# A layer kernel: the down product's first input group split early, its sevens begun later, and one transposed block of x moved by GpSimd's DMA queue

## The chip, the cores and the metric

The kernel runs on one core of one Trainium2 chip. The metric is the device time of one execution in microseconds (us). TensorE (PE) multiplies matrices, VectorE (DVE), ScalarE (ACT) and GpSimd (POOL) work on elements, and SyncE (SP) issues most of the DMAs. Each engine works through its own queue in order; an instruction at the head of a queue that waits for a semaphore holds up all that stands behind it.

## The reference

One layer of a hybrid encoder: SEQ = 256 rows, D_MODEL = 2048, D_FF = 5632, all in float32, batch and depth 1. What matters here are the two half feed-forward products:

```python
def swiglu(h, w_gate, w_up, w_down):
    return (jax.nn.silu(h @ w_gate) * (h @ w_up)) @ w_down

x = x + 0.5 * swiglu(rms_norm(x, ffn1_norm), ffn1_w_gate, ffn1_w_up, ffn1_w_down)
h = rms_norm(x, mix_norm)
proj = h @ w_in              # u | q | k | v
...                          # state space group, attention group, output projection: x += ...
x = x + 0.5 * swiglu(rms_norm(x, ffn2_norm), ffn2_w_gate, ffn2_w_up, ffn2_w_down)
gate = sigmoid(rms_norm(x, ple_norm) @ w_ple_gate)
e = (p @ w_ple_proj) * gate
x = x + rms_norm(e, ple_post_norm)
```

## The kernel before

**Products in three passes.** Each float32 operand is split in a rounded high part (hi, by a copy on ScalarE, L168) and the rest (lo, by a subtract on VectorE, L171). A product is hi by hi, lo by hi and hi by lo, all summed in PSUM: lines L286, L287 and L291 of `gemm_half`, twelve matmuls of 128x512 for a "half" (two row blocks of 128 of the weights, both blocks of 128 rows of x). The names in the profile are whi and wlo for weights, nhi, nlo, hhi, hlo for activations, ahi, alo for prepared quarters. Weights come in tiles of 1 MB (`raw`, three buffers, issued by SP at L275), each of which feeds two halves.

**Gate and up.** `ffn` runs over 11 blocks of 512 hidden columns (f = 0 to 10). A block multiplies x by w_gate and w_up; the later blocks (`pair`) form the first quarter of the inner dimension by a scheme of seven quarter products ("sevens", L301 and L305) instead of eight, from weights in the tiles dg and du, and the rest plainly in `rest`. The end of a pair is L523 (VectorE adds the up sums from PSUM) and L526 (times the gate). The result is turned by a 32x32 transpose on VectorE (L203, into `mid`) and written by sixteen small DMAs of SP (`turn_quarters`, L217) to a tensor `hidden` in DRAM, from which the down product reads it transposed.

**Down.** The third product of the feed-forward multiplies the 5632 hidden columns, in 11 groups of 512, by w_down, for two pairs of column blocks of x (p = 0 and 1). `seven` names the groups that go by sevens, (0, 4) and (0, 4, 7); the others are plain, in an order where both blocks of the pair (c = 0, 1) take each group in turn, except for the last `cut` groups: those go through c = 0 first and then backward through c = 1. Group 1 is thus the first plain group. For a plain group `act` loads the hidden values (hf, L582) and splits them into hhi and hlo; only two groups are held, so some are read again in the backward part. `left` (L617 and splits) prepares the quarters of hidden values for the sevens, `right` (L629, tiles up and low) the weights. The units of the sevens are spread between the plain halves, from half `lead` to half `span`; `merge` adds their sums to x. When a block of x is done (L719), `nxt.block` prepares it for the next stage.

**The next stage's input.** `Normed.block` squares x for the norm (L404) and, for the first three of four blocks, turns it: VectorE transposes (L203, `mid`), sixteen small DMAs of SP move the 32-row strips (L217, h<-mid), and `parted` splits the turned block by ScalarE (nhi, L178) and VectorE (nlo, L180). The last block is transposed by TensorE (L387). After the first product the next stage is the input projection w_in, which runs beside loads for the state space part (L991, six tiles of 512 KB); after the second it is w_ple_gate.

**The order.** `put_off(n, fn)` traces a function n steps later; every half is a step. The program is traced in that order; a planner then places the instructions in each engine's queue by its own estimate of when their inputs are ready, with the traced order as the priority, and inserts the semaphores. So an instruction can stand in a queue at another place than its line suggests; only instructions marked with `pin` keep behind what was traced before them on their engine. Tiles of one tag share a fixed number of buffers (bufs); a new one waits until an older one has been read for the last time. hhi and hlo have two buffers; in the first feed-forward these also hold t1, t2, t4 and kept of a pair, in the second the first two blocks of x.

Of the kernel before, what the change touches and what calls it, by code (L numbers as in the profile page):

```python
# [26 lines left out]
NB = 512  # L27
# [6 lines left out]
def layer_kernel(ctx: ExitStack, tc: tile.TileContext, a: dict, shapes: dict, out: bass.AP):  # L34
# [61 lines left out]
    def start(g):  # L96
        beside.append(g)
        return g
# [106 lines left out]
            src.rearrange("p (f q b) -> p f q b", f=nk, q=4),  # L205
        )

    def turn_quarters(out, mid, steps):

        def g():
            for _ in range(steps):
                yield
            for i in range(4):
                for q in range(4):
                    nc.sync.dma_start(  # L217
                        out[32 * q : 32 * q + 32, :, i], mid[32 * i : 32 * i + 32, q]
                    )
                yield  # L220

        return start(g())
# [135 lines left out]
    class Normed:  # L358
# [8 lines left out]
            self.ss = [small(ND) for _ in range(TT)]  # L367
            self.r = None

        def block(self, n, steps=(6, 11)):  # L370
            if self.laid:
                ps = self.laid(n)
            elif n < self.early:

                mid = com("mid")[:, :1024].rearrange("p (q t f b) -> p q t f b", q=4, t=TT, b=32)
                out = com("h")
                for t in range(TT):
                    turn_blocks(mid, xt[t][n], t, 0, 4)
                turn_quarters(out.rearrange("p (t i f b) -> p t i f b", t=TT, i=4, f=4), mid, steps[0])
                put_off(steps[1], self.parted, n, out.rearrange("p (g f b) -> p f g b", f=4, b=32))  # L380
                put_off(1, self.squares, n)
                return
            else:
                ps = aux()
                for t in range(TT):
                    for j in range(4):
                        pin(nc.tensor.transpose(  # L387
                            ps[:, j * T + t * P : j * T + (t + 1) * P], xt[t][n][:, j * P : (j + 1) * P], ident
                        ))
            self.parted(n, ps.rearrange("p (j s) -> p j s", j=4))  # L390
            if not self.laid:
                put_off(1, self.squares, n)
# [30 lines left out]
    def ffn(i, xn, nxt, bg=None):  # L423
# [21 lines left out]

        first_pair = (early if bg else 0) + 1
        spare = "h" if bg else "n"
        left, right = [], {}

        def fetch(f, steps=6):  # L450


            def g():
                dg, du = (
                    get(hp, s, 4 * NB).rearrange("p (j n) -> p j n", j=4) for s in ("dg", "du")
                )
                for d, w in ((dg, wg), (du, wu)):
                    nc.sync.dma_start(d, w[:NB, f * NB : (f + 1) * NB].rearrange("(j p) n -> p j n", p=P))
                b11, b21, b12, b22 = dg[:, :2], dg[:, 2:], du[:, :2], du[:, 2:]
                t1, t2, t4, kept = (  # L460
                    actp.tile([P, 1024], F32, tag=spare + s, name=uid("t"), bufs={"n": 4, "h": 2}[spare])
                    for s in ("hi", "lo", "hi", "lo")
                )
                t1, t2, t4 = (t.rearrange("p (j n) -> p j n", j=2) for t in (t1, t2, t4))
                right[f] = b11, b21, b22, t1, t2, b12, t4, kept
                for _ in range(steps):
                    yield
                for o, x, y in ((t1, b12, b11), (t2, b22, t1), (b12, b22, b12), (t4, b21, t2)):
                    nc.vector.tensor_tensor(out=o, in0=x, in1=y, op=ALU.subtract)
                    yield  # L470

            start(g())

        def rest(ps, w, f, starts):
            for k0 in range(4, KD, 4):
# [8 lines left out]
        def pair(f, prefetch):  # L484

            (a11, a12, a22), (s1, s2, s3, s4) = left[0]
            b11, b21, b22, t1, t2, t3, t4, kept = right.pop(f)
            x, a, y = acc(), acc(), acc()
            o6, o7 = kept[:, :NB], kept[:, NB:]
            o1, o5 = get(hp, "o1", NB), get(hp, "o5", NB)  # L490
            todo = [
                (x, s2, t2, o6), (a, a11, b11, o1), (y, s1, t1, o5), (x, s3, t3, o7), (a, a12, b21, None),
                (y, s4, b22, None), (x, a22, t4, None),
            ]
            runs = []
            for i, (ps, l, r, o) in enumerate(todo):
                while len(runs) < min(i + 3, len(todo)):
                    n = len(runs)
                    runs.append(product(*todo[n][:3], todo[n][3] is not None and n != 3))
                runs[i]()  # L500
                if o is not None:
                    nc.scalar.copy(o, ps)
                if i % 2 or i == 6:
                    step()
            if prefetch:
                fetch(f + 1)

            def sums():
                nc.vector.tensor_tensor(out=o6, in0=o6, in1=o1, op=ALU.add)
                nc.vector.tensor_tensor(out=o7, in0=o7, in1=o1, op=ALU.add)  # L510
                nc.vector.tensor_tensor(out=o7, in0=o7, in1=o5, op=ALU.add)

            put_off(3, sums)
            rest([a, x], wg, f, ())
            sg = com("sg")
            nc.scalar.activation(sg[:, :NB], a, AF.Silu, scale=xn.rs(0))
            nc.vector.tensor_tensor(out=sg[:, NB:], in0=x, in1=o1, op=ALU.add)
            nc.scalar.activation(sg[:, NB:], sg[:, NB:], AF.Silu, scale=xn.rs(1))
            z = acc()
            rest([y, z], wu, f, (1,))  # L520
            hh = com("h")
            for ps, o in ((y, o6), (z, o7)):
                nc.vector.tensor_tensor(out=o, in0=ps, in1=o, op=ALU.add)  # L523
            for t, o in enumerate((o6, o7)):
                sl = slice(t * NB, (t + 1) * NB)
                nc.vector.scalar_tensor_tensor(  # L526
                    out=hh[:, sl], in0=o, scalar=xn.rs(t), in1=sg[:, sl], op0=ALU.mult, op1=ALU.mult
                )
            put_off(2, turned, hp, f, hh)
# [40 lines left out]
            put_off(2, turned, hp, f, hh)  # L570

        pools.close()
        down(wd, hT, nxt)

    def down(w, hT, nxt):

        nk = F // P // 4
        kept = {}
# [44 lines left out]
        def right(pool, g, n0):  # L623
# [16 lines left out]
            start(g_())  # L640
            return b

        with phase("down") as pool:
            for p in range(ND // 2):
                seven = ((0, 4), (0, 4, 7))[p]
                n0 = 2 * p * NB
                banks = []
                begun = set()
                v1, v7, v6, v5 = (u[:, c * NB : (c + 1) * NB] for u in (aux(), aux()) for c in range(2))
                plain = [g for g in range(nk) if g not in seven]  # L650
                cut = len(plain) - (4 if p else 2)
                order = [(g, c) for g in plain[:cut] for c in range(2)]
                order += [(g, 0) for g in plain[cut:]] + [(g, 1) for g in plain[cut:][::-1]]
                ready, acts = {}, {}

                def units(g):

# [23 lines left out]

                work = all_units()
                n_units, done, halves_done = 7 * len(seven), 0, 0
                lead, span = 4, (28, 22)[p]
                if p == 0:
                    left(pool, seven[0])
                ready[seven[0]] = right(pool, seven[0], n0)
                banks += [acc() for _ in range(4)]
                for g, c in order:
                    if g not in acts:  # L690
# [4 lines left out]
                    for half in list(weight_halves(w, 4 * g, 4, n0 + c * NB)):  # L695
                        keys = (2 * c, 2 * c + 1)
                        starts = tuple(t for t in range(TT) if keys[t] not in begun)
                        begun.update(keys)
                        gemm_half(
                            [banks[k] for k in keys], (acts[g], half), range(TT), starts, end and half[0] == 1,  # L700
                            skip_group_check=True,
                        )
                        step()
                        halves_done += 1
                        due = min(n_units, max(0, (halves_done - lead) * n_units // (span - lead)))
                        while done < due:
                            next(work)
                            done += 1
                            if done % 7 == 2 and done // 7 + 1 < len(seven):
                                ready[seven[done // 7 + 1]] = right(pool, seven[done // 7 + 1], n0)  # L710
                            if (p, done) in ((0, 1), (1, 7)):
                                left(pool, seven[done // 7 + 1])
                            if done == n_units:
                                finish(work)
                                merge(p, v1, v7, v6, v5)
                    if end:
                        n = 2 * p + c
                        for t in range(TT):
                            nc.vector.scalar_tensor_tensor(  # L719
                                out=xt[t][n], in0=banks[2 * c + t], scalar=0.5, in1=xt[t][n], op0=ALU.mult, op1=ALU.add  # L720
                            )
                        put_off(0, nxt.block, n, (4, 9)) if n == ND - 2 else put_off(2, nxt.block, n)

    def merge(p, v1, v7, v6, v5):

# [795 lines left out]
```

## Time and profile before

| | before |
|---|---|
| median of 3 runs | 1892.97 us (1892.61 to 1893.03) |
| the profiled execution | 1891.06 us |
| its span, first to last instruction | 1889.3 us |
| TensorE busy | 1868.1 us, 99% of the span |
| VectorE busy | 1412.9 us, 75% |
| ScalarE busy | 1068.8 us, 57% |
| GpSimd busy | 30.6 us, 2% |
| DMA | 425.65 MB, mean 225 GB/s |
| mean granted clock of TensorE | 0.996 |

Times in the profile's rows are counted from the span's start. A row of the timeline gives start, duration, engine, line, operation, out<-in, shape and count, and in brackets how long the engine stood idle before it and which instruction released it. "SPq" is the issue of a DMA by SP, not its transfer. The first product's down stage begins at 495 us and ends at 736 us, the second product's begins at 1539 us and ends at 1779 us.

### The profile page before, as it was taken

To read this page: it belongs to the slowest core of one execution; us is meant where nothing else is said; L and a number is where in the kernel's file an instruction comes from. 1 tells how busy PE (TensorE), PEld (TensorE's weight loads), DVE (VectorE), ACT (ScalarE), POOL (GpSimd) and SP (SyncE) were. 2 spreads that over 40 slices of the span, in tenths; PEclk is the share of its full clock that TensorE was granted. 3 is DMA by queue.
4 is the path that set the end of the run, shared out by engine and by line. 5 is a ranking of instruction groups with operands and counts; after the bars stand their busy time and mean duration, and the time that the engine had idled before them with its cause. 6 is when DMAs were issued, how large, how long until landed. Compare 5 with 4: busy or idle time off the path is not lost.

```text
span 1889.3 us, 24210 instructions
## 1 busy us (share of the span) xinstructions
PE 1868.1 (99%) x8998; PEld 1539.4 (81%) x8998; DVE 1412.9 (75%) x1898; ACT 1068.8 (57%) x1325; POOL 30.6 (2%) x48
## 2 busy tenths in 40 slices
PE   9999999999999999999999999999999999999998
PEld 7888888888788887888898888888888877888886
DVE  8985766777778886686566877777777778888755
ACT  7456665555455665455785555555555545566654
POOL 0000000000000000010010000000000000000000
PEclk9999999999999999999999999999999999999999
DMA  8777877675887757675547556666656588775653
GB/s 322 233 241 251 270 245 246 203 237 175 281 279 269 237 178 257 232 250 189 199 136 255 192 199 202 220 223 200 201 179 229 174 281 280 272 235 190 226 201 122
DMA packets 268214, 425.65 MB, mean 225 GB/s; under 512 B 17728, under 2 KB 88640, under 8 KB 267968
## 3 DMA queue, kind: packets, MB, share of 16 engines
q1 hardware_dynamic: 255472, 409.06, 65.2%
q10 hardware_dynamic: 12624, 15.04, 2.2%
q8 instruction: 70, 1.15, 0.2%
q14 instruction: 48, 0.39, 0.1%
HBM read 392.59 MB, written 26.21 MB: 222 GB/s over the span
## 4 chain that ended last, share of the span: by engine, by line
PE 95%; DMA 2%; DVE 1%; ACT 1%; issue 0%; SPq 0%; DVEq 0%; ACTq 0%
PE acc L286 26%; PE acc L287 26%; PE acc L291 26%; PE acc L301 6%; PE acc L305 3%; PE aux L301 2%; PE aux L305 1%; DMA hf<-hidden 1%; DMA rot<-scr_rot 0%; PE aux L1008 0%; DVE wlo L171 0%; PE acc L1287 0%; PE acc L1278 0%; PE acc L1282 0%; DMA raw<-in_w_in 0%
## 5 line engine op out<-in xcount | busy, mean ns | idle before, releaser
L168 ACT CAST whi<-raw 128x1024 fp32r<-128x1024 f32 x570 | 595.0, 1053 | 536.6 <-PE acc L287 421.1
L171 DVE TENSOR_TENSOR wlo<-raw,whi 128x1024 fp32r<-128x1024 f32 x570 | 687.5, 1222 | 250.7 <-ACT whi L168 250.0
L286 PE MATMUL acc<-whi,nhi 128*128 128x512 f32 x1504 | 590.6, 393 | 5.6 <-ACT whi L168 4.8
L287 PE MATMUL acc<-whi,nlo 128*128 128x512 f32 x1504 | 586.5, 390 | 0.0
L291 PE MATMUL acc<-wlo,nhi 128*128 128x512 f32 x1504 | 403.5, 389 | 0.0
L286 PEld LDWEIGHTS acc<-whi,nhi 128*128 128x128 f32 x1504 | 282.8, 188 | 67.8 <-ACT whi L168 5.7
L291 PEld LDWEIGHTS acc<-wlo,nhi 128*128 128x128 f32 x1504 | 282.4, 188 | 59.0
L287 PEld LDWEIGHTS acc<-whi,nlo 128*128 128x128 f32 x1504 | 283.0, 188 | 57.8
L287 PE MATMUL acc<-whi,hlo 128*128 128x512 f32 x736 | 287.6, 391 | 6.8 <-DVE hlo L171 6.8
L286 PE MATMUL acc<-whi,hhi 128*128 128x512 f32 x736 | 288.1, 391 | 0.0
L291 PE MATMUL acc<-wlo,hhi 128*128 128x512 f32 x736 | 198.4, 391 | 0.8 <-DVE wlo L171 0.8
L287 PEld LDWEIGHTS acc<-whi,hlo 128*128 128x128 f32 x736 | 138.5, 188 | 37.3 <-DVE hlo L171 7.6
L291 PEld LDWEIGHTS acc<-wlo,hhi 128*128 128x128 f32 x736 | 138.2, 188 | 32.1 <-DVE wlo L171 3.6
L286 PEld LDWEIGHTS acc<-whi,hhi 128*128 128x128 f32 x736 | 138.5, 188 | 30.5
L171 DVE TENSOR_TENSOR wlo<-t,whi 128x1024 fp32r<-128x1024 f32 x72 | 87.8, 1220 | 49.9 <-ACT whi L168 49.7
L168 ACT CAST whi<-t 128x1024 fp32r<-128x1024 f32 x72 | 75.7, 1052 | 75.4 <-PE acc L287 57.3
L168 ACT CAST hhi<-hf 128x1024 fp32r<-128x1024 f32 x38 | 39.7, 1044 | 23.1 <-DMA hf<-hidden 23.1
L171 DVE TENSOR_TENSOR wlo<-dg,whi 128x1024 fp32r<-128x1024 f32 x28 | 34.2, 1222 | 19.9 <-ACT whi L168 19.9
L168 ACT CAST whi<-dg 128x1024 fp32r<-128x1024 f32 x28 | 29.3, 1048 | 33.5 <-PE acc L287 22.4
L171 DVE TENSOR_TENSOR hlo<-hf,hhi 128x1024 fp32r<-128x1024 f32 x38 | 46.3, 1218 | 1.8 <-ACT hhi L168 1.8
L301 PE MATMUL acc<-whi,shi 128*128 128x512 f32 x112 | 44.5, 397 | 0.0
L301 PE MATMUL acc<-whi,slo 128*128 128x512 f32 x112 | 44.1, 394 | 0.0
(319 smaller groups left out, 1792.6 us busy)
## 6 DMA issues: line engine op xcount, KB each, us to landing
raw<-in_ffn_w_up SPq DMA_DIRECT2D x74, 1024.0 KB, 5.8
raw<-in_ffn_w_gate SPq DMA_DIRECT2D x72, 1024.0 KB, 5.3
raw<-in_ffn_w_down SPq DMA_DIRECT2D x68, 1024.0 KB, 6.4
raw<-in_w_in SPq DMA_DIRECT2D x32, 1024.0 KB, 5.6
hf<-hidden SPq DMA_DIRECT2D x44, 512.0 KB, 5.2
raw<-in_w_out SPq DMA_DIRECT2D x16, 1024.0 KB, 5.7
raw<-in_w_ple_gate SPq DMA_DIRECT2D x16, 1024.0 KB, 5.4
dg<-in_ffn_w_gate SPq DMA_DIRECT2D x14, 1024.0 KB, 5.2
```

Source lines behind the costliest of these rows:

```text
L168: copy = nc.scalar.copy(hi, src)
L171: nc.vector.tensor_tensor(out=lo, in0=src, in1=hi.bitcast(F32), op=ALU.subtract)
L286: nc.tensor.matmul(ps[t], lhsT=lh, rhs=hi[:, j, cols], start=t in starts and j == 0, stop=False, **kw)
L287: nc.tensor.matmul(ps[t], lhsT=ll, rhs=hi[:, j, cols], start=False, stop=False, **kw)
L291: nc.tensor.matmul(ps[t], lhsT=lh, rhs=lo[:, j, cols], start=False, stop=stop and j == 1, **kw)
L301: nc.tensor.matmul(ps, lhsT=l[:, j], rhs=hi[:, j], start=start and i + j == 0, stop=False, skip_group_check=True)
L305: nc.tensor.matmul(ps, lhsT=ahi[:, j], rhs=lo[:, j], start=False, stop=j == 1, skip_group_check=True)
```

## The change

Four things change, all around the down product, and in both feed-forward products:

1. After the sevens of the last gate and up block (`pair` without a block to fetch), `begin_down` loads hidden group 1 into the buffer of dg, and five steps later splits it into hhi and hlo. The down product finds it in `early_acts`.
2. In p = 0 the sevens' units run from half 8 to half 30 instead of 4 to 28; `left` of the first seven is traced after the first half, `right` after the third (both stood before the first). `right` of the first seven of p = 1 is traced at half 31 of p = 0, and the units of p = 1 run from half 2 to 20 instead of 4 to 22.
3. In p = 1 the last 5 plain groups, not 4, go through c = 0 first and then backward through c = 1. So c = 0, which is the third block of x, ends with 10 halves to go instead of 8.
4. The third block of x is turned by DMAs on GpSimd's queue (`nc.gpsimd`) instead of SP's, traced 2 steps after the block instead of 4, and split after 11 steps instead of 9.

```diff
-    def turn_quarters(out, mid, steps):
+    def turn_quarters(out, mid, steps, queue=None):
...
-                    nc.sync.dma_start(
+                    (queue or nc.sync).dma_start(
                         out[32 * q : 32 * q + 32, :, i], mid[32 * i : 32 * i + 32, q]
                     )
...
+        def begin_down():
+
+            hf = get(hp, "dg", 4 * NB)[:, :1024]
+            nc.sync.dma_start(hf.rearrange("p (g f b) -> p g f b", f=4, b=32), hT[0][:, :, 4:, :])
+
+            def halved():
+                early_acts[1] = halves("h")
+                split(
+                    *(u.rearrange("p f (g b) -> p f g b", b=32) for u in early_acts[1]),
+                    hf.rearrange("p (g f b) -> p f g b", f=4, b=32),
+                )
+
+            put_off(5, halved)
...
             if prefetch:
                 fetch(f + 1)
+            else:
+                begin_down()
...
+        sevens = ((0, 4), (0, 4, 7))
         with phase("down") as pool:
-            for p in range(ND // 2):
-                seven = ((0, 4), (0, 4, 7))[p]
+            ready = {}
+            for p, seven in enumerate(sevens):
...
-                cut = len(plain) - (4 if p else 2)
+                cut = len(plain) - (5 if p else 2)
...
-                ready, acts = {}, {}
+                acts = {} if p else early_acts
...
-                lead, span = 4, (28, 22)[p]
-                if p == 0:
-                    left(pool, seven[0])
-                ready[seven[0]] = right(pool, seven[0], n0)
+                lead, span = ((8, 30), (2, 20))[p]
...
                         halves_done += 1
+                        if (p, halves_done) == (0, 1):
+                            left(pool, seven[0])
+                        if (p, halves_done) == (0, 3):
+                            ready[seven[0]] = right(pool, seven[0], n0)
+                        if p == 0 and halves_done == 4 * len(plain) - 5:
+                            ready[sevens[1][0]] = right(pool, sevens[1][0], 2 * NB)
...
-                        put_off(0, nxt.block, n, (4, 9)) if n == ND - 2 else put_off(2, nxt.block, n)
+                        put_off(0, nxt.block, n, (2, 11), nc.gpsimd) if n == ND - 2 else put_off(2, nxt.block, n)
```

More of the change, by code (lines that the diff above doesn't have):

```diff
@@ L368, in __init__, with block @@
             self.r = None
-        def block(self, n, steps=(6, 11)):
+        def block(self, n, steps=(6, 11), queue=None):
             if self.laid:
@@ L378, in block @@
                     turn_blocks(mid, xt[t][n], t, 0, 4)
-                turn_quarters(out.rearrange("p (t i f b) -> p t i f b", t=TT, i=4, f=4), mid, steps[0])
+                turn_quarters(out.rearrange("p (t i f b) -> p t i f b", t=TT, i=4, f=4), mid, steps[0], queue)
                 put_off(steps[1], self.parted, n, out.rearrange("p (g f b) -> p f g b", f=4, b=32))
@@ L447, in ffn @@
         spare = "h" if bg else "n"
-        left, right = [], {}
+        left, right, early_acts = [], {}, {}
         def fetch(f, steps=6):
@@ L572, in ffn, with down @@
         pools.close()
-        down(wd, hT, nxt)
-    def down(w, hT, nxt):
+        down(wd, hT, nxt, early_acts)
+    def down(w, hT, nxt, early_acts):
         nk = F // P // 4
```

## The prediction

> **What bounds the kernel.** I read the page first (busy times), then TensorE's own waits, then the order of time around each of those waits.
>
> ```profile
> span 1889.3 us, 24210 instructions
> PE 1868.1 (99%) x8998; PEld 1539.4 (81%) x8998; DVE 1412.9 (75%) x1898; ACT 1068.8 (57%) x1325; POOL 30.6 (2%) x48
> PE acc L287 <- DVE hlo L171: 6.8, 2, 3.4
> PE acc L286 <- ACT whi L168: 4.8, 2, 4.4
> ```
>
> TensorE is the bound: outside its busy time there are 21 us in the span. The last two rows (engine, line, released by: total us, times, longest) name its two long kinds of wait: twice 3.4 us for hlo, once 4.4 for whi. The change takes no arithmetic out of TensorE, so it can win only such waits and what follows from them.
>
> ```profile
> 494.36 1.07 PE L291 MATMUL acc<-wlo,nhi 128*128 128x512 f32 x4
> 495.27 0.39 PE L286 MATMUL acc<-whi,hhi 128*128 128x512 f32 x1
> 499.04 0.50 PE L287 MATMUL acc<-whi,hlo 128*128 128x512 f32 x1 [3.39 <-DVE hlo L171]
> 740.55 1.07 PE L291 MATMUL acc<-wlo,nhi 128*128 128x512 f32 x4
> 746.01 0.80 PE L286 MATMUL acc<-whi,nhi 128*128 128x512 f32 x1 [4.40 <-ACT whi L168]
> 1538.87 0.39 PE L286 MATMUL acc<-whi,hhi 128*128 128x512 f32 x1
> 1542.65 0.50 PE L287 MATMUL acc<-whi,hlo 128*128 128x512 f32 x1 [3.39 <-DVE hlo L171]
> 1562.82 1.20 PE L291 MATMUL acc<-wlo,hhi 128*128 128x512 f32 x4 [0.43 <-DVE wlo L171]
> 1570.31 1.21 PE L291 MATMUL acc<-wlo,hhi 128*128 128x512 f32 x4 [0.33 <-DVE wlo L171]
> ```
>
> ```profile
> 499.00:503.00 4.00, 3.96 (x11) 3.16 (x12) 4.00 (x6) 0.00 (x0) 0.00 (x0) 0.64 0.59 182
> 746.00:750.00 4.00, 3.98 (x11) 3.18 (x12) 3.65 (x4) 3.28 (x4) 0.00 (x0) 0.59 0.81 278
> 1542.60:1546.60 4.00, 3.95 (x17) 3.11 (x18) 4.00 (x6) 0.04 (x1) 0.00 (x0) 1.00 0.65 206
> ```
>
> In the second fence the columns are stretch and length, then busy time and count of PE, PEld, DVE, ACT, POOL, then granted clock, DMA share, GB/s. I compare starts, since ends are modelled: four matmuls take 494.36 to 495.27, so one takes 0.23 and a half (twelve) 2.73. First down start: 499.04-495.27-0.23 = 3.54 lost, and the clock of 0.64 over the next 4 us loses 4.00x0.36 = 1.44: **4.98**. Start of the input projection: 746.01-740.55-0.91 = 4.55, plus 4.00x0.41 = 1.64: **6.19**. Second down start: 1542.65-1538.87-0.23 = 3.55, full clock after it, plus 0.43 and 0.33 a little later, where VectorE is behind: **4.31**. Together 15.48 us are within this change's reach.
>
> **Part 1: group 1 split beside the last gate and up block.** Why TensorE waits at 495 is seen in the order of VectorE, ScalarE and SP there:
>
> ```profile
> 484.82 1.22 DVE L171 TENSOR_TENSOR wlo<-raw,whi 128x1024 fp32r<-128x1024 f32 x1 [1.50 <-ACT whi L168]
> 495.24 1.29 DVE L523 TENSOR_TENSOR t<-acc,t 128x512 f32<-128x512 f32 x2 [5.80 <-PE acc L291]
> 496.45 1.41 DVE L526 SCALAR_TENSOR_TENSOR h<-t,sm,sg 128x512 f32<-128x512 f32 x2
> 497.77 1.22 DVE L171 TENSOR_TENSOR hlo<-hf,hhi 128x1024 fp32r<-128x1024 f32 x1
> 480.17 0.55 SPq L582 DMA_DIRECT2D hf<-hidden  x1
> 480.82 4.15 SPq L275 DMA_DIRECT2D raw<-in_ffn_w_down  x2
> 489.80 1.05 ACT L168 CAST hhi<-hf 128x1024 fp32r<-128x1024 f32 x1 [4.10 <-DMA hf<-hidden]
> 492.58 2.00 ACT L168 CAST whi<-raw 128x1024 fp32r<-128x1024 f32 x2 [1.73 <-DMA raw<-in_ffn_w_down]
> ```
>
> hlo's operand hhi was there at 490.85, but hlo stands in VectorE's queue behind L523 and L526, which need TensorE's last up product; VectorE idles 5.80 us at the head of that queue. With the split five steps into the pair, hhi (1.05) and hlo (1.22) are moved, not added, into halves where VectorE has gaps of 1.50. hf's SP issue (0.55) moves some 20 us forward; a weight load behind it is later by that much. Cost 0 by this cover; 2.3 us per product without it.
>
> Late next is the first wlo. TensorE runs eight matmuls on whi (1.8 us, to 497.1) before it needs wlo. Before, the first sevens' hidden group and its four weight loads stood on SP ahead of that block's weights, which were issued at 480.82 and cast only at 492.58. After the change they come behind them. I expect the weights some 4 us sooner, and their wlo in VectorE's idle 5.80, ahead of L523. At the other block borders, where that is the order, TensorE shows no such wait. If the planner leaves wlo behind L526, it ends at 497.77+1.22 = 498.99, and 1.9 us of each start stays. I take 0 and keep 1.9 for the rivals. Gain here 4.98 and 3.55.
>
> **Part 2: the first sevens run over halves 8 to 30 instead of 4 to 28, their left and right loaded after the first and third half.** Nothing is added: 14 units in 22 halves instead of 24.
>
> ```profile
> 1555.00:1573.00 18.00, 17.25 (x75) 13.49 (x74) 18.00 (x22) 11.30 (x13) 0.00 (x0) 1.00 1.02 344
> 1598.00:1745.00 147.00, 146.98 (x640) 119.81 (x639) 123.33 (x124) 86.74 (x99) 0.00 (x0) 1.00 0.72 238
> ```
>
> Early in the down stage VectorE is busy 18 of 18 us and the DMA engines are full; that is where the 0.43 and 0.33 are lost. Later VectorE is at 123.33/147 = 84%; units packed 24/22 closer can lift that to 92% at most, still under full. So the later begin wins 0.76 and the closer packing costs 0; without that cover the 0.76 would come in both products. The second pair of blocks keeps its rate (21 units in 18 halves) two halves earlier, with its first right loaded in advance by four SP issues: 0.
>
> **Part 3: cut 5, not 4, in the last pair of blocks.** One more hidden group is read again in each product: one hf load of 0.5 MB, one hhi, one hlo, in halves without sevens, where the gaps are those of the 1.50 row: 0 by cover, 2.3 us each without.
>
> **Part 4: the third block of x by GpSimd's queue, two steps earlier and, by part 3, two halves earlier.**
>
> ```profile
> 717.61 1.30 DVE L203 STREAM_TRANSPOSE mid<-x 128x512 f32<-128x512 f32 x2
> 718.93 8.41 SPq L217 DMA_DIRECT2D h<-mid  x12
> 727.45 0.52 SPq L275 DMA_DIRECT2D raw<-in_w_in  x1
> 731.49 5.25 SPq L217 DMA_DIRECT2D h<-mid  x4
> 737.50 3.20 SPq L275 DMA_DIRECT2D raw<-in_w_in  x3
> 736.01 0.39 PE L286 MATMUL acc<-whi,nhi 128*128 128x512 f32 x1
> 742.89 1.70 ACT L178 ACTIVATE nhi<-h,gains 128x256 fp32r<-128x256 f32 x4 [7.80 <-DMA h<-mid]
> 744.92 1.99 ACT L168 CAST whi<-raw 128x1024 fp32r<-128x1024 f32 x2 [0.33 <-DMA raw<-in_w_in]
> 718.90:727.40 8.50, 8.50 (x39) 7.02 (x38) 7.54 (x8) 5.06 (x5) 0.00 (x0) 1.00 0.18 41
> 727.40:737.40 10.00, 10.00 (x46) 8.28 (x45) 3.70 (x5) 2.00 (x2) 0.00 (x0) 1.00 0.91 332
> L217 SPq DMA_DIRECT2D h<-mid x16: 585/596/1256, 718.9 to 736.2; - x16
> DMA to landing us min/median/max: 1.8/1.9/10.5
> L997 POOL COPY dec<-rho x8: 612/1564/1667, 703.5 to 841.4; 128x512 f32<-128x512 f32 x8
> ```
>
> SP issues sixteen small copies (the x16 row: ns least, median, most). During the first twelve the DMA engines are at 0.18, and the projection's weights come only behind them at 727.45 and, behind the last four, at 737.50. Without them SP issues these weights as their buffers come free, into the 8.5 idle us. ScalarE stood 7.80 us at nhi for the copies, and whi followed at 744.92, when its weights had landed too. Both reasons go: gain 6.19. At the end of the second product TensorE shows no such wait: gain 0.
>
> The price is GpSimd's issue, which no row shows. Nearest are SP's issues of these same copies, 0.59 to 1.26 us; the longest GpSimd instruction here takes 1.67. Ends: 0.59 and 1.67; I take x = 1.26, the longest of the nearest row. Transposes end at 718.91, 17.1 before the stage's end at 736.01; two halves earlier make it 22.6. Sixteen issues end 16x-22.6 after the stage's end, land 1.9 later, nhi takes 1.70, a whi 1.05, and TensorE comes to the second quarter at 5.5: no wait up to 16x = 23.4, x = 1.46. At 1.26 there are 3.2 us to spare; 0.59 wins nothing more; 1.67 costs 2x(26.7-23.4) = 6.6 over both products. Queued behind the copies on GpSimd are only the dec fills; for the copies themselves nhi waits, and behind it on ScalarE whi.
>
> The Trainium skill, SBUF — State Buffer, section "SBUF: two separate sides", says that GpSimd cannot write a DMA's descriptors while VectorE holds the port they share. The same section limits this to VectorE's two-port fast mode; no run so far shows a DMA from GpSimd. The Trainium skill, DMA: Bandwidth & Descriptors, "Anatomy of one DMA", gives about 2.0 us fixed per DMA on this path; were that paid one after the other, x = 2.0, the sum would be an estimated +1.7 instead of -15.48.
>
> **The sum.** -4.98-6.19-4.31 = -15.48. The profiled execution took 1891.06, its span 1889.3; the median of the three runs is 1892.97, 1.9 above the profiled one. Against the median 1877.5; the next span near 1873.8.
>
> **Rivals.**
> - The subtract stays late (wlo behind L526): 3.8 us stay, 1881.3. For it: that order before; against it: the idle 5.80. Chance 0.12.
> - The projection's weights are late anyway: SP's other loads fill the DMA engines (332 GB/s in the row above) ahead of them, 6.19 stays, 1883.7. Against it: 8.5 idle us just before. Chance 0.10.
> - The split does not come early, so the change does not do what it says: its buffers come free late, or hf waits on SP behind the hidden copies. Both down starts stay: 1877.5+9.3 = 1886.8. Chance 0.06.
> - GpSimd's issue lies between 1.46 and 1.95: up to 15.48 lost, about 1884 at 1.67. Chance 0.06.
> - The other side: GpSimd is held up by VectorE at each copy. The dec row is for it: the same fill takes 0.61 at best and 1.67 at most, 1.06 longer when VectorE works beside it. x = 1.26+1.06 = 2.32; nhi then heads ScalarE's queue at both ends: 2x(37.1-23.4)-15.48 = +11.9, 1904.9. It decides from x = 1.95. Against it: that fill moves its 128x512 elements itself, a DMA's issue does not, and VectorE is busy only 3.70 of 10 us in the second stretch above. Chance 0.07.
> - A new wait where none was foreseen, by the planner's changed order: 0.06, half of it slower.
>
> **Numbers.** The forecast, all three waits gone, has 0.53: 1877.5, its own range 1875 to 1880. 0.2% is 3.8 us, about what a measurement of this kernel can tell from no change. Faster: the forecast and the first four rivals, 0.87; same: half of the last, 0.03; slower: the blocked GpSimd and the other half, 0.10. The range takes in all the faster cases: 1874 to 1889.
>
> **What will show it.** Part 1: no wait of TensorE for hlo, wlo before L523 on VectorE at both down starts, no clock of 0.64 after. Part 2: no waits of 0.3 to 0.4 for wlo in the first 40 us. Part 3: two more hhi and hlo. Part 4: the projection's first two weight loads issued within some 10 us of the transposes, no 4.4 wait for whi. GpSimd's issue rows give x: under 1.46 I am right there; over 1.95 the sign is wrong.

## The result and the profile after

The changed kernel takes 1885.26 us (median of six runs, 1884.41 to 1887.12) where the kernel before took 1892.79 beside it: a ratio of 0.9962, 95% interval 0.9949 to 0.9975. It is faster by 7.5 us, less than half of the 15.5 that were forecast. The profiled execution took 1887.12 us, the longest of the six.

First the page after (span and busy times), then TensorE's waits after (engine, line, released by: total us, times, longest):

```profile
span 1885.3 us, 24252 instructions
PE 1868.8 (99%) x8998; PEld 1542.1 (82%) x8998; DVE 1415.6 (75%) x1900; ACT 1070.7 (57%) x1327; POOL 47.6 (3%) x80
```

```profile
PE acc L286 <- ACT hhi L168: 5.7, 2, 2.9
...
PE acc L287 <- DVE hlo L171: 1.6, 2, 1.0
...
PE acc L286 <- ACT whi L168: 0.5, 1, 0.5
PE acc L291 <- DVE wlo L171: 0.3, 1, 0.3
```

TensorE's busy time is 1868.8 us after 1868.1, so again the waits decide. Those of before are gone: for hlo no longer twice 3.4 but 1.6 in all, and at another place; for whi no longer 4.8 but 0.5. In their place stands one that was not there before: twice 2.9 us for hhi, and hlo right behind it. The stretches of the after trace show where (columns as in the prediction):

```profile
480.00:510.00 30.00, 30.00 (x134) 24.87 (x133) 22.86 (x28) 14.61 (x17) 0.00 (x0) 1.00 0.83 277
720.00:738.00 18.00, 14.26 (x50) 10.95 (x49) 7.66 (x10) 7.35 (x10) 1.22 (x3) 0.81 0.68 242
1500.00:1580.00 80.00, 80.00 (x353) 66.01 (x353) 63.79 (x70) 42.16 (x47) 0.00 (x0) 1.00 0.88 291
1755.00:1775.00 20.00, 16.40 (x60) 12.65 (x59) 10.13 (x12) 8.10 (x11) 2.65 (x6) 0.83 0.71 242
```

Both starts of the down product (first and third row) are full now, at full clock. Both ends (second and fourth row) have a hole (TensorE is busy 14.26 of 18.00 us and 16.40 of 20.00) and a slowed clock (0.81 and 0.83). The order of time around the first hole, on TensorE, ScalarE, GpSimd and SP:

```profile
724.39 1.07 PE L291 MATMUL acc<-wlo,hhi 128*128 128x512 f32 x4
728.24 0.50 PE L286 MATMUL acc<-whi,hhi 128*128 128x512 f32 x1 [2.79 <-ACT hhi L168]
729.69 0.80 PE L287 MATMUL acc<-whi,hlo 128*128 128x512 f32 x1 [0.95 <-DVE hlo L171]
...
716.43 1.06 ACT L168 CAST whi<-raw 128x1024 fp32r<-128x1024 f32 x1 [0.72 <-PE acc L287]
725.40 0.91 ACT L178 ACTIVATE nhi<-h,gains 128x256 fp32r<-128x256 f32 x2 [7.92 <-DMA h<-mid]
726.22 1.03 ACT L168 CAST whi<-raw 128x1024 fp32r<-128x1024 f32 x1
727.15 1.04 ACT L168 CAST hhi<-hf 128x1024 fp32r<-128x1024 f32 x1
728.10 0.90 ACT L178 ACTIVATE nhi<-h,gains 128x256 fp32r<-128x256 f32 x2
...
708.87 4.89 POOL L217 DMA_DIRECT2D h<-mid  x9 [608.33 <-DVE mid L203]
715.47 3.24 POOL L217 DMA_DIRECT2D h<-mid  x6 [1.72 <-DMA h<-mid]
719.40 0.53 POOL L217 DMA_DIRECT2D h<-mid  x1 [0.69 <-DMA h<-mid]
...
711.59 0.53 SPq L598 DMA_DIRECT2D hf<-hidden  x1
712.73 16.17 SPq L275 DMA_DIRECT2D raw<-in_w_in  x3
```

The planner put two of the four nhi (the third x block's split) ahead of the hhi of the last hidden group that is read again. They stand at the head of ScalarE's queue for 7.92 us until GpSimd's copies have landed at 725.3; hhi, whose values SP had asked for at 711.59, is cast only at 727.15. With it stands a whi, the high part of the weights for the same half: it is done at 726.22+1.03 = 727.25, also behind TensorE's need near 725.30. The wait is put down to hhi because hhi comes last. The rows of the copies themselves, after:

```profile
L217 POOL DMA_DIRECT2D h<-mid x16: 533/538/679, 708.9 to 719.4; - x16
  ACT nhi L178: 7.9, 1
  POOL h L217: 2.4, 2
DMA to landing us min/median/max: 1.8/5.5/6.5
```

GpSimd issues a copy in 0.54 us (median; at most 0.68). The copies need 5.5 us from issue to landing, and GpSimd's later issues themselves wait 2.4 us for earlier copies.

### The profile page after: what moved, and what is told of

The parts are those of the page before. It is cut to its first block, busy times and chain, and to the rows that moved or that the text cites. A ratio compares the mean times of both kernels' runs of the same rounds, so it can differ in the third digit from the quotient of the medians.

```text
span 1885.3 us, 24252 instructions
## 1 busy us (share of the span) xinstructions
PE 1868.8 (99%) x8998; PEld 1542.1 (82%) x8998; DVE 1415.6 (75%) x1900; ACT 1070.7 (57%) x1327; POOL 47.6 (3%) x80
## 4 chain that ended last, share of the span: by engine, by line
PE 95%; DMA 2%; DVE 1%; ACT 1%; issue 1%; POOL 0%; SPq 0%; ACTq 0%; POOLq 0%; DVEq 0%
PE acc L286 26%; PE acc L287 26%; PE acc L291 26%; PE acc L301 6%; PE acc L305 3%; PE aux L301 2%; DMA h<-mid 1%; PE aux L305 1%; PE aux L1028 0%; PE acc L1307 0%; PE acc L1302 0%; PE acc L1298 0%; POOL h L217 0%; DVE wlo L171 0%; PE aux L947 0%
## 5 line engine op out<-in xcount | busy, mean ns | idle before, releaser
L217 POOL DMA_DIRECT2D h<-mid x32 | 17.1, 542 | 1360.3 <-DVE mid L203 1355.8
```

What stands on the lines that cost most here:

```text
L217: (queue or nc.sync).dma_start(out[32 * q : 32 * q + 32, :, i], mid[32 * i : 32 * i + 32, q])
```

## The experiments

Each kernel was timed beside the kernel before on the same chip; ratios are to it. Two theories stood first. Theory A: the place of nhi in ScalarE's queue makes the new wait. Theory B: the late landing, or the extra reread, costs wherever nhi stands. The result was neither of the two alone.

**nhi held behind the last hhi** (label pin): the changed kernel, with `pinned` true for the third x block's four copies alone.

```diff
-            nc.scalar.activation(hi[:, j], src[:, j], AF.Copy, scale=scale)
+            copy = nc.scalar.activation(hi[:, j], src[:, j], AF.Copy, scale=scale)
+            if pinned:
+                pin(copy)
```

> The changed kernel, with one thing more: the four scaled copies nhi of the third x block are held on ScalarE behind the casts that were traced before them, so that the hhi of the last hidden group that is read again stands ahead of them. Theory A (the place of nhi in ScalarE's queue makes the new wait): in the changed kernel's trace TensorE lost 3.7 us in gaps and 3.1 us in slow clock behind them at the end of each down stage, 13.6 in both. Without them about 1885.3-13.6 = 1871.7; some of the projection's own wait may come back, so 1872 to 1878. hhi starts within 2 us of its hf, no wait of TensorE for it. Theory B (the late landing of GpSimd's copies, 5.5 us each, is what costs, wherever nhi stands): the wait moves to the projection's start, where nhi or the whi behind it comes late; 1884 to 1887.

1872.65 us, ratio 0.9895 (0.9881 to 0.9908): 12.6 us below the changed kernel's median. ScalarE after, with nhi held (line numbers two higher below this edit):

```profile
719.78 1.04 ACT L168 CAST hhi<-hf 128x1024 fp32r<-128x1024 f32 x1
...
730.62 1.71 ACT L178 ACTIVATE nhi<-h,gains 128x256 fp32r<-128x256 f32 x4
```

hhi is cast at 719.78 instead of 727.15, nhi stands at 730.62 with no idle time before it, and TensorE has neither wait. GpSimd's copies land as late as in the changed kernel (median 5.5), and here that costs nothing: Theory B falls.

**No extra reread** (label cut4): the changed kernel, with cut 4 and the steps that go with it.

```diff
-                cut = len(plain) - (5 if p else 2)
+                cut = len(plain) - (4 if p else 2)
-  put_off(0, nxt.block, n, (2, 11), nc.gpsimd)
+  put_off(0, nxt.block, n, (2, 9), nc.gpsimd)
```

> The changed kernel without the extra reread: cut 4 as before, and the second step count 9 instead of 11, which the shorter loop needs; GpSimd's queue, the early split and the later sevens stay. No hhi is left behind nhi on ScalarE then. Theory A (the wait is that of the last reread group's hhi behind nhi): the wait for hhi goes; the copies begin two halves nearer to the stage's end, about 4 us, so nhi ends some 4 us later and only the projection's first weights can be held up: 1872 to 1880. Theory B (GpSimd's late landing costs as such): the landing is nearer to the projection's start, so the wait at least stays: 1885 to 1890.

1873.63 us, ratio 0.9897 (0.9882 to 0.9912). No hhi is left behind nhi, and the wait is gone, though GpSimd's copies land late here too (median 4.8 us) and nhi stands idle for them for 7.28 us. TensorE's longest wait for a whi, 1.6 us, is at 217.61, in the first gate and up product and not at this place. So the reread matters in the changed kernel by its group, whose whi and hhi are caught behind nhi.

**The copies back on SP's queue** (label sp):

```diff
-  put_off(0, nxt.block, n, (2, 11), nc.gpsimd)
+  put_off(0, nxt.block, n, (2, 11))
```

> The changed kernel with the third x block's small copies back on SP's queue (the earlier steps, the extra reread, the early split and the later sevens stay). In this kernel's order all four nhi stand ahead of the last reread group's hhi on ScalarE. Theory A (place in the queue): the wait for hhi stays and grows, since the last four copies by SP land later than GpSimd's, and the projection's weights stand behind the copies on SP again: 1886 to 1896. Theory C (GpSimd's queue itself, with its landing of 5.5 us, is the cause): with SP's landing of 1.9 us the wait goes: 1876 to 1881.

1882.04 us, ratio 0.9940 (0.9928 to 0.9953). Neither theory has it. ScalarE and SP with the copies on SP's queue, then TensorE's longest kind of wait:

```profile
721.05 1.71 ACT L178 ACTIVATE nhi<-h,gains 128x256 fp32r<-128x256 f32 x4 [5.11 <-DMA h<-mid]
723.74 1.05 ACT L168 CAST hhi<-hf 128x1024 fp32r<-128x1024 f32 x1 [0.98 <-DMA hf<-hidden]
...
708.45 10.29 SPq L217 DMA_DIRECT2D h<-mid  x16
718.84 1.07 SPq L598 DMA_DIRECT2D hf<-hidden  x1
...
PE acc L286 <- ACT whi L168: 5.3, 4, 2.3
```

All four nhi stand ahead of hhi, but their copies land in 1.9 us (median), nhi is through by 722.8, and hhi then waits for its own hf, which SP issued only behind the sixteen copies. What TensorE waits for is not hhi, though, but the whi of the same half: its weights stand behind hf on SP, are issued at 719.95 and cast at 726.85. What this kernel loses against the one with nhi held, 9.4 us, would then come from SP's queue and not from ScalarE's, which the next run tests.

**nhi held and the copies on SP's queue** (label pin_sp): both edits above.

> The kernel with nhi held behind the last hhi, and the third x block's copies on SP's queue instead of GpSimd's. Theory G (GpSimd's queue matters because it takes 10 us of issue off SP, ahead of the last reread group's load and of the weights): the w_down weights and that group come late as in the run with SP's queue, which lost 2.4 us at each down stage's end and 1.5 behind: 1877 to 1882. Theory H (only the place of nhi matters): as with GpSimd's queue, 1872 to 1875.

1881.07 us, ratio 0.9942 (0.9930 to 0.9955), as Theory G has it. With nhi out of the way hhi still comes at 724.01, released by its hf, and the whi at 727.08, released by its weights; TensorE waits 6.6 us in all for whi. So GpSimd's queue is worth 0.9942-0.9895, some 9 us, once nhi is placed well.

**The early split and the later sevens alone** (label parts12): cut 4, SP's queue and the steps (4, 9) as before the change.

> The early split and the later sevens alone: cut 4, the steps 4 and 9 and SP's queue are as before the change. By the prediction's terms both down starts are won, 4.98 + 4.31 = 9.3, and the projection's wait of 6.2 stays: 1892.8-9.3 = 1883.5 (1881 to 1886). If the early split brings less than that, because the slow clock after the stall is not in these terms as counted or another wait follows, 1886 to 1891.

1876.64 us, ratio 0.9915 (0.9901 to 0.9928): 15.9 us won where the terms gave 9.3. Both down starts are full, and the projection's wait is smaller as well, 1.8 us instead of 4.4. SP in this kernel:

```profile
711.23 8.24 SPq L217 DMA_DIRECT2D h<-mid  x12
...
720.14 3.03 SPq L217 DMA_DIRECT2D h<-mid  x4
723.28 0.52 SPq L1011 DMA_DIRECT2D m1r<-scr_m1r  x1
```

The planner now issues the last four copies at 720.14, ahead of the six loads for the state space part; before, they came at 731.49, behind them. So these two parts alone won more than the whole change, and the other two, in its order, gave 8.6 us of it back.

**The early split alone** (label split), the kernel before with only `begin_down` and `early_acts`:

> The kernel before with the early split of the first input group alone; the sevens, their loads, cut 4, the steps and SP's queue as before. Theory D (the parts add up as the prediction has them): both waits for hlo go, 8.5 us, the two waits of 0.3 to 0.4 for wlo and the projection's wait stay: 1892.5-8.5 = 1884 (1882 to 1886). Theory E (the early split and the later sevens need each other, since the sevens' group and weights still stand on SP ahead of the first block's weights): the wait moves from hlo to whi or wlo, and less than half is won: 1888 to 1892.

1885.93 us, ratio 0.9970 (0.9958 to 0.9981). TensorE's wait for wlo with the split alone, then VectorE's order at the first down start:

```profile
PE acc L291 <- DVE wlo L171: 3.6, 2, 1.8
```

```profile
495.51 1.29 DVE L539 TENSOR_TENSOR t<-acc,t 128x512 f32<-128x512 f32 x2 [5.05 <-PE acc L291]
496.71 1.41 DVE L542 SCALAR_TENSOR_TENSOR h<-t,sm,sg 128x512 f32<-128x512 f32 x2
498.04 2.35 DVE L171 TENSOR_TENSOR wlo<-raw,whi 128x1024 fp32r<-128x1024 f32 x2
```

hlo is early, but wlo takes its place behind L539 and L542 (the L523 and L526 of before): 1.8 us twice instead of 3.4. The time lies at the upper end of Theory D's range, and some 6 us are won where D has 8.5; but the wait has moved from hlo to wlo, as E has it. So neither holds as it stands.

**The later sevens alone** (label sevens), the kernel before with the units from 8 to 30 and the moved `left` and `right`:

> The kernel before with the later sevens alone (8 to 30, left and right after the first and third half, the second pair's right in advance); no early split, cut 4, the steps and SP's queue as before. The two parts together, run before this, won 15.9 where their terms gave 9.3. Theory D (terms add up): 0.76, so 1891 to 1892.5, and the projection's wait of 6 us stays. Theory F (the surplus comes from here: with other loads at another time the planner places the last four small copies ahead of the projection's coefficient loads, and its wait falls from 5.8 to about 2): 0.76 + 4 to 6, 1886 to 1889.

1878.46 us, ratio 0.9927 (0.9914 to 0.9939): 13.5 us. Theory D gave 0.76 and F up to 6.8; both are far off. What F names does happen: SP issues the last four copies at 720.27, ahead of the six loads, and the projection's wait falls from 4.4 to 1.7 us. But both down starts are won as well. VectorE and SP with the later sevens alone:

```profile
486.02 1.22 DVE L171 TENSOR_TENSOR hlo<-hf,hhi 128x1024 fp32r<-128x1024 f32 x1
490.27 1.23 DVE L171 TENSOR_TENSOR wlo<-raw,whi 128x1024 fp32r<-128x1024 f32 x1 [1.45 <-ACT whi L168]
495.31 1.29 DVE L523 TENSOR_TENSOR t<-acc,t 128x512 f32<-128x512 f32 x2 [2.80 <-PE acc L291]
...
476.51 0.59 SPq L582 DMA_DIRECT2D hf<-hidden  x1
477.21 0.84 SPq L275 DMA_DIRECT2D raw<-in_ffn_w_down  x1
...
481.49 2.38 SPq L629 DMA_DIRECT2D up<-in_ffn_w_down  x2
```

With up and low behind the first loads of hf and the weights on SP, these are there early enough for hlo (486.02) and wlo (490.27) both to stand ahead of L523, with no early split at all.

**The extra reread and the moved copies alone** (label copies), the kernel before with cut 5 and GpSimd's queue at the steps (2, 11):

> The kernel before with the other two parts alone: the extra reread (cut 5), and the third x block moved by GpSimd's queue at the steps 2 and 11; no early split, no later sevens. In this kernel's order on ScalarE the last reread group's hhi stands ahead of all four nhi. Theory A (place in the queue): no wait for hhi, the projection's wait of 6.2 goes, both down starts stay: 1886.3 (1884 to 1889). Theory B (the extra reread or the late landing costs wherever nhi stands): 1890 to 1897.

1884.84 us, ratio 0.9965 (0.9951 to 0.9978): 7.1 us, and the projection's wait is gone. In this kernel the last hhi stands ahead of all four nhi with no pin. So the bad order belongs to none of the four parts by itself.

**No early split, nhi held and not held** (labels nosplit_pin and nosplit): the changed kernel without `begin_down`.

> The changed kernel without the early split, with the four nhi held behind the casts traced before them. Theory I (the later sevens alone bring the first product's hlo forward, since its hidden group is no longer behind four weight loads on SP, and the early split adds only the 0.4 us waits for wlo that the run with the later sevens still had at 508 and 1542): 1872.65 + 1 to 2 = 1873 to 1875. Theory J (with the copies moved too the split is needed, and a wait of 3.5 us for hlo comes back at each down start): 1877 to 1881.

1874.37 us, ratio 0.9904 (0.9889 to 0.9919): Theory I. Beside the later sevens the early split adds 1.7 us by the medians, which the intervals do not separate from nothing.

> The changed kernel without the early split, nothing held: on ScalarE two nhi stand ahead of the last reread group's hhi, as in the changed kernel. Theory A (place in the queue): TensorE waits for hhi near 725 and 1764 as in the changed kernel, some 13 us over the kernel with the same parts and nhi held behind: 1885 to 1889. If the wait belongs to the early split's own buffers or loads: 1873 to 1876.

1886.53 us, ratio 0.9966 (0.9953 to 0.9978); TensorE waits twice 3.0 us at most for hhi, as in the changed kernel. The bad order comes, then, when the later sevens meet the reread and the moved copies.

**The extra reread alone, on the two first parts** (label reread): parts12 with cut 5.

> The kernel with the early split and the later sevens (1876.6 when timed), with the extra reread (cut 5) added and nothing else; the small copies by SP's queue at the steps 4 and 9. On ScalarE the last hhi stands ahead of the nhi. By the prediction's step (an extra hf, hhi and hlo cost 0 where VectorE has gaps) and Theory A: no wait for hhi, and with the stage's copies two halves sooner the projection's wait of 2.0 us is smaller or gone: 1873 to 1877. Theory B (the extra reread itself costs, 2.3 us a product or more): 1881 to 1888.

1877.91 us, ratio 0.9921 (0.9907 to 0.9935), beside 0.9915 without it: no cost that can be told, which bears out Part 3's 0; but the projection's wait did not shrink either, it is 3.1 us at most.

**The copies shared between both queues** (labels both, with nhi held, and both_free, with nothing held):

```diff
-                    (queue or nc.sync).dma_start(
+                    (queue if queue and q % 2 == 0 else nc.sync).dma_start(
```

> The kernel with nhi held, with the third x block's sixteen copies shared: eight by GpSimd's queue, eight by SP's, in the same stretch beside the same weight loads. It asks why GpSimd's copies took 5.5 us to land where SP's had taken 1.9. Theory K (full DMA engines: SP's copies landed in 1.9 while the engines were at 0.18, GpSimd's in 5.5 while they were at 1.07): SP's eight now land in 3.5 us or more as well, GpSimd's within 1 us of them. Theory L (GpSimd's queue is slow by itself): SP's land in about 1.9, GpSimd's in about 5.5 still. The time: eight issues of 0.6 on SP delay the last reread group's load and the weights by some 5 us, half of what all sixteen did: 1873 to 1878.

1872.94 us, ratio 0.9900 (0.9883 to 0.9916). Copies by GpSimd (first row) and by SP (second row), then the DMA share (next to last column) beside them:

```profile
DMA to landing us min/median/max: 1.8/1.8/1.9
...
DMA to landing us min/median/max: 1.9/2.0/2.1
```

```profile
708.00:712.00 4.00, 4.00 (x19) 3.30 (x19) 4.00 (x5) 3.04 (x3) 3.16 (x6) 1.00 0.29 66
712.00:716.00 4.00, 4.00 (x20) 3.30 (x19) 3.45 (x3) 2.02 (x3) 3.37 (x6) 1.00 0.48 119
```

In the changed kernel the same stretches read:

```profile
708.00:712.00 4.00, 4.00 (x20) 3.30 (x19) 4.00 (x5) 3.01 (x3) 3.13 (x6) 1.00 0.31 85
712.00:716.00 4.00, 4.00 (x19) 3.31 (x18) 3.04 (x4) 2.04 (x3) 2.28 (x6) 1.00 1.08 326
```

SP, busy with its eight copies, issues the weights later, the DMA engines stay at 0.29 to 0.48, and GpSimd's copies land in 1.8 us too. So GpSimd's queue is not slow by itself: the copies land in 5.5 when the weight loads fill the engines (1.08) beside them. Theory L falls; K's numbers do not come, since the eight copies on SP took the load away. What K says is seen in the kernel before: of SP's own sixteen copies there, the last four were issued into engines at 0.91 (the prediction's row of 727.40), and they landed no sooner than GpSimd's:

```profile
L217 SPq DMA_DIRECT2D h<-mid x4: 585/586/597, 731.5 to 736.2; - x4
DMA to landing us min/median/max: 6.4/8.3/10.5
```

Nor is it the number of copies on GpSimd's queue. In the run copies its first copy, with none ahead of it, took 4.3 us beside engines at 0.87 (718 to 722); the first in the changed kernel took 1.8. Last, the question whether the place of nhi alone makes the wait:

> The changed kernel, nothing held, with the sixteen copies shared between GpSimd's and SP's queues. All four nhi stand ahead of the last reread group's hhi on ScalarE. With nhi held, the shared copies landed in 1.8 to 2.1 us and the last by 715. Theory A1 (the place of nhi is enough for the wait): near 1885. Theory A2 (place and late landing are needed together: with the last copy down by 715, nhi is through by 717.5, before hhi's own values are there and 8 us before TensorE needs them): no wait for hhi, 1872 to 1875.

1872.97 us, ratio 0.9897 (0.9879 to 0.9915). ScalarE with the copies shared and nothing held:

```profile
715.09 1.71 ACT L178 ACTIVATE nhi<-h,gains 128x256 fp32r<-128x256 f32 x4
720.21 1.06 ACT L168 CAST whi<-raw 128x1024 fp32r<-128x1024 f32 x1 [3.41 <-DMA raw<-in_ffn_w_down]
721.17 1.05 ACT L168 CAST hhi<-hf 128x1024 fp32r<-128x1024 f32 x1
```

All four nhi stand ahead of hhi and hold nothing up: the copies are down before nhi's turn. Theory A2: the wait needs both, nhi ahead of hhi and copies that land late. Either one mended gives 1873.

## Why the prediction was wrong

The sign held, the size did not. Against the kernel before, a version with all of the change's parts and no new wait wins 19.9 us (nhi held); the forecast was 15.5; the change as it stands won 7.5, because it brought a wait worth 12.6.

- **The bound and the three waits: right.** All three are gone after. They were under-sized: with nothing new in the way the kernel wins some 4 us more than 4.98 + 6.19 + 4.31. The two profiled executions, before and with nhi held, tell where, by TensorE's first matmul of each stage. The first down product falls from 240.74 us (495.27 to 736.01) to 235.01 (495.36 to 730.37): 5.73 where 4.98 was counted. The way from there to the second down product falls by 6.21, where 6.19 was counted. The second down product falls from 240.58 us (1538.87 to 1779.45) to 234.81 (1527.02 to 1761.83): 5.77 where 4.31 was counted. So the second down start is the term most short; what it left out was not looked into.
- **Part 1: the effect was right, the cause was misplaced.** The split was credited with 8.5 us, and wlo ahead of L523 was ascribed in passing to the sevens' weights coming later. The split alone leaves wlo behind L539, 1.8 us at each start, just the 1.9 us that the rival kept; the sevens' loads out of the way bring hlo and wlo forward without the split. That both starts are won, as the sum has it, is partly luck: the change held Part 2 as well.
- **Part 2: 0.76 was mis-sized; it measured 13.5 alone.** The term looked at VectorE's load in the sevens and left out the remark in Part 1 on SP's order. The same four loads cost both down starts. The 13.5 holds most of what Part 1 was credited with and some of the projection's wait, which Part 4 was credited with, so it does not add to them.
- **Part 3: 0 was right as a cost by itself** (1877.91 beside 1876.64). What was left out is where its hhi would stand.
- **Part 4, the step that failed.** The projection's gain was real, and x = 0.54 us is even below the low end of 0.59 to 1.67. Two assumptions beside it were not. The copies' landing, 1.9, was the median of SP's copies, twelve of which ran while the DMA engines were at 0.18. The same row gives 10.5 at most: that is one of the last four, issued into engines at 0.91, none of which landed in under 6.4. The same step forecast that SP would move the weights into just the microseconds of the new copies, and then the engines are at 1.08 and the landing is 5.5. And "behind it on ScalarE whi" looked only at the projection: the whi and hhi of the group that Part 3 adds came to stand behind nhi. By the prediction's own landing, the last copy issued at 719.40 would have been down at 719.93+1.9 = 721.8 and hhi done 0.91+1.03+1.04 later, at 724.8, 0.5 us ahead of TensorE's need near 725.3 (724.39+0.91): no wait for hhi even in this order, and about 0.5 us for hlo, 1.22 behind it. So the landing, with the place, is the term: 12.6 us over both ends.
- **The rivals.** "A new wait by the planner's changed order", at 0.06 and with no price, is what came. GpSimd held up by VectorE, at 0.07, did not come: its issues took 0.53 to 0.68 us with VectorE busy 4.00 of 4.00 us (the row of 708 above). The Trainium skill, SBUF — State Buffer, section "SBUF: two separate sides", keeps that blocking to VectorE's two-port mode. This trace shows none of the blocking; whether VectorE ran in that mode here it does not tell.
- **The rule on the DMA's fixed time.** The landing of 1.8 us with free engines is near the 2.0 us that the Trainium skill, DMA: Bandwidth & Descriptors, section "Anatomy of one DMA", gives. The same page, section "Queues, rings and completion order", says that each DMA engine takes packets in turn from the queues that have work for it. The 5.5 us at a DMA share of 1.08 agree with that.

Open is why the planner puts nhi ahead of hhi when the sevens begin later and not otherwise; its estimates were not looked into.

## What to carry to other kernels

When a transfer is moved to make room for others, take its landing time from a stretch that is as full as the one it will then run in, not from the emptier stretch it leaves: here the median was 1.9 us and the most 10.5, and the most was the better guide. Then list every instruction that may stand behind its consumer on an in-order engine, those that the same change adds above all, with the time each is needed. And when one change has several parts, time each part alone before crediting it: here one part of four brought 13.5 us, and two others, added to the first two, took 8.6 of 15.9 us away again.

## What was not expected of the hardware

GpSimd issued a 32 KB copy in 0.54 us, quicker than SP's 0.60 (medians). After its first nine issues it waited 1.72 us, and after the next six 0.69, for earlier copies to land. That is the program's doing and not a limit of the queue: the trace's semaphores show that these copies use eight of them in turn, so that the ninth copy waits for the first to land and the tenth for the second. So the landing time also lengthened the issuing: sixteen copies took 11.1 us from first to last (708.87 to 719.93), where 16x0.54 is 8.6. The same small copies landed in 1.8 us with the DMA engines at 0.29 to 0.48 and in 5.5 at 1.08, on the same queue; on SP's queue they took 1.9 at 0.18 and 8.3 at 0.91 (all medians).
